# Expert weights from 64-column products, with the second one-hot stored tokens innermost

## The chip, the cores and the metric

The kernel runs on one core of a Trainium2 chip. The metric is device time in microseconds (us) from launch to end, taken as the median of several runs; the profile is one execution, taken by the hardware profiler, and shows the span from its first to its last instruction. Engines are named as in the profile: PE is TensorE's products, PEld its weight loads, DVE is VectorE, ACT is ScalarE, POOL is GpSimd and SP is SyncE. Lines are those of the kernel before, unless the text says otherwise.

## The reference, cut to what matters

The program is two transformer blocks over 256 tokens of width 1024. The first ends in a layer with 16384 small experts, laid out as a grid of 128 by 128. For each token and each of 8 heads, routing picks 16 experts, each by a pair of indices, and a softmax weight for each. So a token has 128 (index, index, weight) triples. The layer is

```python
z = jnp.einsum('thkd,td->thk', ub, hb)           # ub: the picked rows of u
a = (jax.nn.gelu(z.astype(jnp.float32)) * gb).astype(hb.dtype)
return jnp.einsum('thk,thkd->td', a, jnp.take(v, eb, axis=0))
```

All values are float32.

## The kernel before, in words

The kernel gathers nothing. It computes z for all experts densely, in 128 chunks of 128 experts by 256 tokens (`z_chunks`, line 1201: the weights of a chunk are loaded, split into a high and a low part by ACT, line 166, and DVE, line 167, and 24 products of 256 columns give z, lines 190 to 192; ACT applies the gelu on the way out of PSUM, line 987). A chunk has one second index and all 128 first indices on the partitions. The z of 32 chunks stand in one tile, a slice, so there are four slices, 0 to 3. Each z is multiplied by its expert's weight for that token, which is zero nearly everywhere, and `out_chunks` then multiplies the result with v, chunk by chunk, in products of 512 columns (lines 261 to 263, after another split by lines 268 and 269).

The weights come from `weights_of(s, n)`, which makes those of n slices from slice s on: it is called with (0, 1), (1, 2) and (3, 1). It goes over the tokens in 32 blocks of TB = 8. For each token the weight matrix, first index by second index, is a product over the token's 128 triples, which lie on the partitions: the one-hot of the first index, times the one-hot of the second index scaled by the weight. Both are f16; the weight g is split into a high and a low f16 part (i = 0 and 1, `gT`), so that two products, added up in PSUM, keep its precision. A block does this:

- DVE compares a table of numbers `io16` with the first indices and writes the one-hot `os`, tokens innermost (line 1166); ACT turns it to `o1`, one token's 128 columns in a row (line 1169).
- DVE compares `row16`, a row of the numbers 0 to 127, with the second indices and writes `o2`, tokens outermost (line 1172): m = 32 n columns a token.
- DVE multiplies `o2` with both parts of the weight into `og` (line 1176).
- PE does, for each of the 8 tokens and both parts, a weight load of `o1` and a product of m columns (line 1191) into the bank `g`, of which there are two.
- DVE multiplies z in place with what stands in the bank, one instruction a slice (line 1194).

`weights_of` is a generator that yields after making a block's operands and after the block's products; the operands are made one block ahead. The loops over chunks advance it: 1.5 steps a chunk while the chunks 50 to 95 of z are computed (slice 0), 1.05 while the first 32 chunks go out and the last 32 of z are computed (slices 1 and 2), and 1.05 while chunks 32 to 95 go out (slice 3). The engines run their instructions in the order in which they were recorded, so a block's instructions stand between those of the chunks. In `spread` (line 1111 and 1112) DVE writes the two parts of the weight to `gT`, tokens outermost. Line 973 fills `row16` once from `io16`, and the small product in `spread` (line 1099) puts the weights in order; neither is in the blocks.

Of the kernel before, what the change touches and what calls it, by code (L numbers as in the profile page):

```python
# [8 lines left out]
F32 = mybir.dt.float32  # L9
F32R = mybir.dt.float32r  # L10
F16 = mybir.dt.float16
# [3 lines left out]
ALU = mybir.AluOpType  # L15
# [7 lines left out]
TB = 8  # L23
# [90 lines left out]
def body(ctx: ExitStack, tc: tile.TileContext, a: dict):  # L114
    nc = tc.nc
    V, A, G, T, SY = nc.vector, nc.scalar, nc.gpsimd, nc.tensor, nc.sync

    def pool(name, space=None, stack=None, bufs=1):
        kw = {"space": space} if space else {}
        return (stack or ctx).enter_context(tc.tile_pool(name=name, bufs=bufs, reuse_waits="tile", **kw))  # L120
# [6 lines left out]
    def mmt(n=256):  # L127
        return pmm.tile([128, 512], F32, tag="mm", name="mm", bufs=2)[:, :n]
# [9 lines left out]
    def C(n, i=None, w=128):  # L138
        t, o, ww = CST[n]
        return cst[t][:, o:o + ww] if i is None else cst[t][:, o + i * w:o + i * w + w]  # L140
# [312 lines left out]
    with ExitStack() as p1:  # L453
# [320 lines left out]
        for t in ORD2.split():  # L774
            n = int(t[1])
# [86 lines left out]
        for j, w in enumerate(chunks(a["wo"], range(4))):  # L862
            ps = mmt()
# [12 lines left out]
        for j, w in enumerate(chunks(a["wga"], range(4))):  # L876
            ps = mmt()
# [18 lines left out]
        for j, w in enumerate(chunks(a["wgm"], range(4))):  # L896
            ps = mmt()
# [12 lines left out]
        for j in range(8):  # L910
            ps = mmt()
# [7 lines left out]
        for j in range(8):  # L919
            ps = mmt()  # L920
# [27 lines left out]
    with ExitStack() as p2:  # L948
        zp = pool("zp", stack=p2)
        zq = [zp, zp]  # L950
        m2 = pool("m2", stack=p2)
# [4 lines left out]
        def gt():  # L956
            return pgp.tile([128, 512], F32, tag="g", name="g", bufs=2)
# [10 lines left out]
        io16 = m2.tile([128, 128, TB], F16, name="io16")  # L968
        A.dma_start(out=io16, in_=a["io16"].rearrange("p (i t) -> p i t", t=TB))
        idxT = m2.tile([128, 2, 256], F16, name="idxT")  # L970
        gT = m2.tile([128, 256, 2], F16, name="gT")
        row16 = m2.tile([128, 128], F16, name="row16")
        V.tensor_copy(row16, io16[:, :, 0])

        rst = ExitStack()
        rp = pool("rp", stack=rst)
# [111 lines left out]
        def spread(t):  # L1088

            ex = rp.tile([128, 8, 16], F32, tag="ex", name="ex", bufs=2)  # L1090
            V.tensor_sub(ex, gw[t], gw[t][:, :, 0:1].to_broadcast([128, 8, 16]))
            A.activation(ex, ex, AF.Exp)
            sm = rp.tile([128, 2, 8], F32, tag="sm", name="sm", bufs=2)
            V.tensor_reduce(out=sm[:, 0, :], in_=ex, axis=AX.X, op=ALU.add)
            V.reciprocal(sm[:, 1, :], sm[:, 0, :])
            gp = rp.tile([128, 2, 16, 4], F32, tag="gp", name="gp", bufs=2)
            for q in range(2):
                hs = slice(4 * q, 4 * q + 4)
                V.tensor_mul(gp[:, q].rearrange("p k h -> p h k"), ex[:, hs],
                             sm[:, 1, hs, None].to_broadcast([128, 4, 16]))  # L1100
            yield 1.3
            ts_ = slice(t * 128, (t + 1) * 128)
            pt = gt()[:, :256]
            for i in range(2):
                T.transpose(pt[:, i * 128:(i + 1) * 128], fi[t][:, i, :], C("ident"))
            V.tensor_copy(idxT[:, :, ts_], pt.rearrange("p (i t) -> p i t", i=2))
            pg = gt()
            T.transpose(pg[:, 0:128], gp.rearrange("p q k h -> p (q k h)"), C("ident"))
            gs = rp.tile([128, 128], F32, tag="gs", name="gs", bufs=1)
            A.activation(gs, pg[:, 0:128], AF.Copy, scale=GS)  # L1110
            V.tensor_copy(gT[:, ts_, 0], gs)
            V.tensor_sub(gT[:, ts_, 1], gs, gT[:, ts_, 0])
            yield 1.0

        def routing():
            for hq in range(4):
                for t in range(2):
                    while (hq, t) not in scs:
                        yield
                    yield from route(t, hq, scs[hq, t])  # L1120
                if hq % 2:
                    for t in range(2):
                        yield from select(t, hq // 2)
                        if hq == 3:
                            yield from spread(t)
# [31 lines left out]
        def weights_of(s, n):  # L1157

            m = 32 * n

            def made_of(b):
                ts_ = slice(b * TB, (b + 1) * TB)
                os = op_.tile([128, 128, TB], F16, tag="os", name="os", bufs=1)
                V.tensor_tensor(out=os, in0=io16, in1=idxT[:, 0, None, ts_].to_broadcast([128, 128, TB]),  # L1166
                                op=ALU.is_equal)
                o1 = op_.tile([128, TB, 128], F16, tag="o1", name="o1", bufs=2)
                A.copy(o1, os.rearrange("p n t -> p t n"))  # L1169
                o2 = op_.tile([128, TB * 64], F16, tag="o2", name="o2", bufs=1)[:, :TB * m]  # L1170
                o2 = o2.rearrange("p (t n) -> p t n", t=TB)
                V.tensor_tensor(out=o2, in0=row16[:, None, 32 * s:32 * s + m].to_broadcast([128, TB, m]),
                                in1=idxT[:, 1, ts_, None].to_broadcast([128, TB, m]), op=ALU.is_equal)
                og = op_.tile([128, TB * 128], F16, tag="og", name="og", bufs=2)[:, :2 * TB * m]
                og = og.rearrange("p (t i n) -> p t i n", t=TB, i=2)
                V.tensor_tensor(out=og, in0=o2[:, :, None, :].to_broadcast([128, TB, 2, m]),  # L1176
                                in1=gT[:, ts_, :, None].to_broadcast([128, TB, 2, m]), op=ALU.mult)
                return o1, og

            blocks = S // TB  # L1180
            next_ = made_of(0)
            yield
            for b in range(blocks):
                o1, og = next_
                if b + 1 < blocks:
                    next_ = made_of(b + 1)
                    yield
                ps = gt()[:, :TB * m].rearrange("p (t n) -> p t n", t=TB)
                for t in range(TB):
                    for i in range(2):  # L1190
                        T.matmul(ps[:, t], lhsT=o1[:, t, :], rhs=og[:, t, i], start=i == 0, stop=i == 1)  # L1191
                for q_ in range(n):
                    zz = zt[s + q_][:, :, b * TB:(b + 1) * TB]
                    V.scalar_tensor_tensor(out=zz, in0=ps[:, :, 32 * q_:32 * q_ + 32].rearrange("p t n -> p n t"),  # L1194
                                           scalar=1.0 / GS, in1=zz, op0=ALU.mult, op1=ALU.mult)
                yield

# [36 lines left out]
        op_ = pool("op", stack=p2)  # L1234
        zq.append(op_)
        bg = [weights_of(0, 1)]
        z_chunks(ZR, 96, bg, NW)
        drain(bg)
        acc = [[pacc.tile([128, 512], F32, tag=f"acc{2 * t + c}", name="acc") for c in range(2)] for t in range(2)]
        rt = m2.tile([128, 2, 5], F32, name="rt")  # L1240

        bg = [weights_of(1, 2)]
        out_chunks(0, 32, bg, NX)
        z_chunks(96, 128, bg, NX)
        drain(bg)
        bg = [weights_of(3, 1)]
        out_chunks(32, 96, bg, NY)
        drain(bg)
# [10 lines left out]
    with ExitStack() as p3:  # L1259
# [48 lines left out]
        for j in range(8):  # L1308
            if j < 4:
                ps = pss[j]  # L1310
            else:
                ps = mmt()
# [53 lines left out]
        for j in range(4):  # L1366
            ps = mmt()
# [8 lines left out]
            for i in range(1, 4):  # L1376
                V.scalar_tensor_tensor(out=u2[:, j, :], in0=pad[:, i:i + 256], scalar=K("wc2", 4 * i + j),
                                       in1=u2[:, j, :], op0=ALU.mult, op1=ALU.add)
        gl = big("gl", F32, 4)
        for j in range(4):  # L1380
            ps = mmt()
# [7 lines left out]
            for i in range(2):  # L1389
                s_ = slice(64 * i, 64 * i + 64)  # L1390
                V.scalar_tensor_tensor(out=q2[s_, 2 * j + i, :], in0=qk[s_, j, :], scalar=lru[s_, 12:13],
                                       in1=rb[s_], op0=ALU.mult, op1=ALU.mult)
# [102 lines left out]
        for n in range(32):  # L1495
            if n < 4:
                ps = pss[n]
            else:
                ps = mmt()
# [139 lines left out]
```

## Time and profile before

| what | us |
|---|---|
| median of 3 runs (1453.45 to 1455.68) | 1454.52 |
| the profiled execution | 1454.12 |
| its span, first to last instruction | 1452.3 |
| PE busy | 1429.2 |
| PEld busy | 1312.1 |
| DVE busy | 1134.0 |
| ACT busy | 923.0 |

Busy time is the time in which at least one instruction of an engine was under way. PE's products overlap, since one starts before the one ahead of it has ended, so that a PE that is busy all the time need not be at its peak; the distance between the starts of two products says more than their duration. Idle time of an engine that is not the bottleneck costs nothing.

### The profile page before, as it was taken

The page shows a single profiled execution, that of the slowest core. Times are in us where ns is not written, and L with a number is a line of the kernel's source. Part 1 is how long each engine was busy: PE and PEld are TensorE (multiplying, and loading weights), DVE is VectorE, ACT ScalarE, POOL GpSimd, SP SyncE. Part 2 cuts the span into 40 slices and gives each one's busy share as a digit, 9 for nine tenths or more (in the row PEclk, how much of TensorE's full clock was granted, in tenths as well). Part 3 has the DMA queues.
Part 4 walks back from the last instruction along what each step waited for, and adds up shares of the span by engine and source line. Part 5 has one row for each costly group of instructions (what it writes and reads, how often), then busy time and mean ns, then how long its engine had stood idle before and what let it go on. Part 6 is the DMA issues. An engine that isn't in the chain of part 4 may idle for free.

```text
span 1452.3 us, 27093 instructions
## 1 busy us (share of the span) xinstructions
PE 1429.2 (98%) x10984; PEld 1312.1 (90%) x10984; DVE 1134.0 (78%) x2208; ACT 923.0 (64%) x1322; POOL 7.8 (1%) x11
## 2 busy tenths in 40 slices
PE   7999999999999999999999999999999999999998
PEld 6999999988999999998779997777788899989997
DVE  4979987668999878888998888888855778565554
ACT  4655565456444578887777777777744669454542
POOL 0000000010000000000000000000000000000000
PEclk9999999999999999999999999999999999999999
DMA  8757785553655555544545555555555543255552
GB/s 320 294 188 236 280 334 195 174 174 126 206 174 173 188 165 171 175 151 170 174 162 169 192 164 180 170 172 173 172 190 179 194 173 140 88 204 174 174 179 82
DMA packets 40301, 268.67 MB, mean 185 GB/s; under 512 B 4720, under 2 KB 5488, under 8 KB 9584
## 3 DMA queue, kind: packets, MB, share of 16 engines
q1 hardware_dynamic: 39168, 264.67, 52.9%
q10 hardware_dynamic: 1008, 2.27, 0.5%
q8 instruction: 86, 1.41, 0.4%
q14 instruction: 39, 0.32, 0.1%
HBM read 265.87 MB, written 1.05 MB: 184 GB/s over the span
## 4 chain that ended last, share of the span: by engine, by line
PE 92%; DVE 5%; ACT 2%; DMA 0%; issue 0%; DVEq 0%; SPq 0%; ACTq 0%
PE mm L190 16%; PE mm L192 15%; PE mm L191 15%; PE acc L261 11%; PE acc L262 11%; PE acc L263 11%; PE g L1191 3%; DVE wl L167 1%; DVE scr L471 1%; PE psb L606 1%; PE mm L226 1%; PE mm L225 1%; PE acc L190 1%; PE mm L230 1%; PE mm L209 1%; PE acc L192 1%
## 5 line engine op out<-in xcount | busy, mean ns | idle before, releaser
L166 ACT CAST wh<-raw 128x1024 fp32r<-128x1024 f32 x444 | 465.2, 1050 | 423.0 <-PE mm L191 217.9
L167 DVE TENSOR_TENSOR wl<-raw,wh 128x1024 fp32r<-128x1024 f32 x444 | 541.3, 1222 | 160.0 <-ACT wh L166 154.2
L190 PE MATMUL mm<-hh,wh 128*128 128x256 f32 x1800 | 512.7, 285 | 0.0
L192 PE MATMUL mm<-hh,wl 128*128 128x256 f32 x1800 | 507.2, 282 | 0.0
L191 PE MATMUL mm<-hl,wh 128*128 128x256 f32 x1800 | 505.6, 281 | 0.0
L190 PEld LDWEIGHTS mm<-hh,wh 128*128 128x128 f32 x1800 | 339.2, 188 | 2.0
L191 PEld LDWEIGHTS mm<-hl,wh 128*128 128x128 f32 x1800 | 339.9, 189 | 0.9
L192 PEld LDWEIGHTS mm<-hh,wl 128*128 128x128 f32 x1800 | 340.2, 189 | 0.0
L261 PE MATMUL acc<-wh,ah 128*128 128x512 f32 x512 | 205.4, 401 | 0.0
L262 PE MATMUL acc<-wh,al 128*128 128x512 f32 x512 | 201.9, 394 | 0.0
L263 PE MATMUL acc<-wl,ah 128*128 128x512 f32 x512 | 201.5, 394 | 0.0
L1169 ACT COPY o<-os 128x1024 f16<-128x1024 f16 x96 | 196.8, 2050 | 0.0
L263 PEld LDWEIGHTS acc<-wl,ah 128*128 128x128 f32 x512 | 96.2, 188 | 22.3
L261 PEld LDWEIGHTS acc<-wh,ah 128*128 128x128 f32 x512 | 96.2, 188 | 20.7
L262 PEld LDWEIGHTS acc<-wh,al 128*128 128x128 f32 x512 | 96.1, 188 | 20.5
L1194 DVE SCALAR_TENSOR_TENSOR z<-g,z 128x256 f32<-128x256 f32 x128 | 51.2, 421 | 43.3 <-PE g L1191 43.2
L1166 DVE TENSOR_TENSOR os<-io,idxT 128x1024 f16<-128x1024 f16 x96 | 66.3, 691 | 23.2 <-ACT o L1169 22.4
L1176 DVE TENSOR_TENSOR og<-o,gT 128x512 f16<-128x512 f16 (+1 forms) x96 | 82.6, 860 | 0.1
L1191 PEld LDWEIGHTS <-o 128*128 128x128 f16 x1536 | 46.5, 96 | 15.4 <-issue 12.2
L1191 PE MATMUL g<-og,o 128*128 128x32 f16 (+1 forms) x1536 | 56.6, 182 | 0.0
L269 DVE TENSOR_TENSOR al<-z,ah 128x256 fp32r<-128x256 f32 x128 | 53.5, 419 | 1.1 <-ACT ah L268 1.1
L471 DVE SCALAR_TENSOR_TENSOR scr<-araw,crow 128x1024 f32<-128x1024 f32 x43 | 52.4, 1218 | 0.2
(449 smaller groups left out, 1854.4 us busy)
## 6 DMA issues: line engine op xcount, KB each, us to landing
raw<-in_uT_dram SPq DMA_DIRECT2D x64, 1024.0 KB, 4.9
raw<-in_ev_dram SPq DMA_DIRECT2D x64, 1024.0 KB, 4.9
araw<-in_wada_dram SPq DMA_DIRECT2D x16, 1024.0 KB, 4.9
raw<-in_wup_dram SPq DMA_DIRECT2D x16, 1024.0 KB, 4.9
raw<-in_wdn_dram SPq DMA_DIRECT2D x16, 1024.0 KB, 4.9
raw<-in_wcxb_dram SPq DMA_DIRECT2D x12, 1024.0 KB, 4.9
raw<-in_wout_dram SPq DMA_DIRECT2D x8, 1024.0 KB, 4.8
raw<-in_wq_dram SPq DMA_DIRECT2D x8, 1024.0 KB, 4.8
```

The source lines that it names most:

```text
L166: by.copy(wh, raw) if by is A else by.tensor_copy(wh, raw)
L167: last = on.tensor_sub(wl, raw, wh)
L190: T.matmul(ps, lhsT=wh, rhs=xh, start=start, stop=False, skip_group_check=skip)
L191: T.matmul(ps[:, :n], lhsT=wh, rhs=xl, start=False, stop=False, skip_group_check=skip)
L192: return T.matmul(ps, lhsT=wl, rhs=xh, start=False, stop=stop, skip_group_check=skip)
L261: T.matmul(acc[t][c], lhsT=xh[:, ts_], rhs=wh[:, cs], start=first and n == 0, stop=False)
L262: T.matmul(acc[t][c], lhsT=xl[:, ts_], rhs=wh[:, cs], start=False, stop=False)
L263: T.matmul(acc[t][c], lhsT=xh[:, ts_], rhs=wl[:, cs], start=False, stop=last and n == len(steps) - 1)
L471: return V.scalar_tensor_tensor(out=scr, in0=raw, scalar=0.5, in1=crow, op0=ALU.mult, op1=ALU.mult, accum_out=ada[:, j:j + 1])
L1169: A.copy(o1, os.rearrange("p n t -> p t n"))
L1176: V.tensor_tensor(out=og, in0=o2[:, :, None, :].to_broadcast([128, TB, 2, m]), in1=gT[:, ts_, :, None].to_broadcast([128, TB, 2, m]), op=A ...
L1191: T.matmul(ps[:, t], lhsT=o1[:, t, :], rhs=og[:, t, i], start=i == 0, stop=i == 1)
```

## The change

In all slices, `o2`, `og` and `gT` now stand with tokens innermost: `o2` is compared straight out of `io16`, `row16` is gone, and the multiplication by the weight is two instructions, one for each part. PE therefore reads one token's columns of `og` with a step of TB = 8 elements of f16.

In slices 0 and 3 (n = 1), one product a token now takes both parts of the weight beside each other, as 64 columns, where there were two products of 32 columns added up in PSUM. The two halves are added afterwards: ACT copies the second half out of PSUM to a tile `both`, DVE adds the first half to it, and the update of z reads `both`. In slices 1 and 2 (n = 2) there are two products of 64 columns, as before.

```diff
--- before.py
+++ after.py
@@ -968,9 +968,7 @@
         io16 = m2.tile([128, 128, TB], F16, name="io16")
         A.dma_start(out=io16, in_=a["io16"].rearrange("p (i t) -> p i t", t=TB))
         idxT = m2.tile([128, 2, 256], F16, name="idxT")
-        gT = m2.tile([128, 256, 2], F16, name="gT")
-        row16 = m2.tile([128, 128], F16, name="row16")
-        V.tensor_copy(row16, io16[:, :, 0])
+        gT = m2.tile([128, 2, 256], F16, name="gT")
 
         rst = ExitStack()
         rp = pool("rp", stack=rst)
@@ -1108,8 +1106,8 @@
             T.transpose(pg[:, 0:128], gp.rearrange("p q k h -> p (q k h)"), C("ident"))
             gs = rp.tile([128, 128], F32, tag="gs", name="gs", bufs=1)
             A.activation(gs, pg[:, 0:128], AF.Copy, scale=GS)
-            V.tensor_copy(gT[:, ts_, 0], gs)
-            V.tensor_sub(gT[:, ts_, 1], gs, gT[:, ts_, 0])
+            V.tensor_copy(gT[:, 0, ts_], gs)
+            V.tensor_sub(gT[:, 1, ts_], gs, gT[:, 0, ts_])
             yield 1.0
 
         def routing():
@@ -1168,13 +1166,14 @@
                 o1 = op_.tile([128, TB, 128], F16, tag="o1", name="o1", bufs=2)
                 A.copy(o1, os.rearrange("p n t -> p t n"))
                 o2 = op_.tile([128, TB * 64], F16, tag="o2", name="o2", bufs=1)[:, :TB * m]
-                o2 = o2.rearrange("p (t n) -> p t n", t=TB)
-                V.tensor_tensor(out=o2, in0=row16[:, None, 32 * s:32 * s + m].to_broadcast([128, TB, m]),
-                                in1=idxT[:, 1, ts_, None].to_broadcast([128, TB, m]), op=ALU.is_equal)
+                o2 = o2.rearrange("p (n t) -> p n t", t=TB)
+                V.tensor_tensor(out=o2, in0=io16[:, 32 * s:32 * s + m, :],
+                                in1=idxT[:, 1, None, ts_].to_broadcast([128, m, TB]), op=ALU.is_equal)
                 og = op_.tile([128, TB * 128], F16, tag="og", name="og", bufs=2)[:, :2 * TB * m]
-                og = og.rearrange("p (t i n) -> p t i n", t=TB, i=2)
-                V.tensor_tensor(out=og, in0=o2[:, :, None, :].to_broadcast([128, TB, 2, m]),
-                                in1=gT[:, ts_, :, None].to_broadcast([128, TB, 2, m]), op=ALU.mult)
+                og = og.rearrange("p (i n t) -> p i n t", i=2, t=TB)
+                for i in range(2):
+                    V.tensor_tensor(out=og[:, i], in0=o2, in1=gT[:, i, None, ts_].to_broadcast([128, m, TB]),
+                                    op=ALU.mult)
                 return o1, og
 
             blocks = S // TB
@@ -1185,13 +1184,24 @@
                 if b + 1 < blocks:
                     next_ = made_of(b + 1)
                     yield
-                ps = gt()[:, :TB * m].rearrange("p (t n) -> p t n", t=TB)
-                for t in range(TB):
-                    for i in range(2):
-                        T.matmul(ps[:, t], lhsT=o1[:, t, :], rhs=og[:, t, i], start=i == 0, stop=i == 1)
+                if n == 1:
+
+                    ps = gt()[:, :2 * TB * m].rearrange("p (t i n) -> p t i n", t=TB, i=2)
+                    for t in range(TB):
+                        T.matmul(ps[:, t], lhsT=o1[:, t, :], rhs=og[:, :, :, t], start=True, stop=True)
+                    both = op_.tile([128, TB, 32], F32, tag="both", name="both", bufs=1)
+                    A.copy(both, ps[:, :, 1])
+                    V.tensor_tensor(out=both, in0=ps[:, :, 0], in1=both, op=ALU.add)
+                    gs_ = [both]
+                else:
+                    ps = gt()[:, :TB * m].rearrange("p (t n) -> p t n", t=TB)
+                    for t in range(TB):
+                        for i in range(2):
+                            T.matmul(ps[:, t], lhsT=o1[:, t, :], rhs=og[:, i, :, t], start=i == 0, stop=i == 1)
+                    gs_ = [ps[:, :, 32 * q_:32 * q_ + 32] for q_ in range(n)]
                 for q_ in range(n):
                     zz = zt[s + q_][:, :, b * TB:(b + 1) * TB]
-                    V.scalar_tensor_tensor(out=zz, in0=ps[:, :, 32 * q_:32 * q_ + 32].rearrange("p t n -> p n t"),
+                    V.scalar_tensor_tensor(out=zz, in0=gs_[q_].rearrange("p t n -> p n t"),
                                            scalar=1.0 / GS, in1=zz, op0=ALU.mult, op1=ALU.mult)
                 yield
 
```

The order of PE's instructions in a block of slice 0, before, from the last product of a chunk to the first weight loads of the block (`o` is the turned one-hot, `g` the bank); 14 more pairs follow before the next product of a chunk.

```order
L192 MATMUL mm<-hh,wl 128x256
L1191 LDWEIGHTS o_6483
L1191 MATMUL g<-og,o_6483 128x32
L1191 LDWEIGHTS o_6483
L1191 MATMUL g<-og,o_6483 128x32
```

After the change, in the same place; 6 more pairs follow.

```order
L192 MATMUL mm<-hh,wl 128x256
L1191 LDWEIGHTS o_6481
L1191 MATMUL g<-og,o_6481 128x64
L1191 LDWEIGHTS o_6481
L1191 MATMUL g<-og,o_6481 128x64
```

A block of slice 0 has 16 pairs before and 8 after, at the same place between the chunks; the products are twice as wide.

ACT in slice 0, before: the cast `wh` of a chunk's weights, its gelu into `z`, and the turned one-hot `o` of a block.

```order
L166 CAST wh<-raw 128x1024
L987 ACTIVATE z<-mm 128x256
L166 CAST wh<-raw 128x1024
L987 ACTIVATE z<-mm 128x256
L1169 COPY o_6839<-os 128x1024
L166 CAST wh<-raw 128x1024
L987 ACTIVATE z<-mm 128x256
```

After:

```order
L166 CAST wh<-raw 128x1024
L985 ACTIVATE z<-mm 128x256
L166 CAST wh<-raw 128x1024
L985 ACTIVATE z<-mm 128x256
L1193 COPY both<-g 128x256
L1167 COPY o_6818<-os 128x1024
L166 CAST wh<-raw 128x1024
L985 ACTIVATE z<-mm 128x256
```

The copy to `both`, which waits for the block's products, stands between the gelu and the `o` of the next block.

DVE in slice 0, before: the update of z, `og` of the next block, the low part `wl` of a chunk's weights, the one-hot `os` and the second one-hot `o`.

```order
L1194 SCALAR_TENSOR_TENSOR z<-g,z 128x32x8
L1176 TENSOR_TENSOR og<-o_7131,gT 128x512
L167 TENSOR_TENSOR wl<-raw,wh 128x1024
L1166 TENSOR_TENSOR os<-io_3918,idxT 128x1024
L1172 TENSOR_TENSOR o_7188<-row_3922,idxT 128x256
L1194 SCALAR_TENSOR_TENSOR z<-g,z 128x32x8
```

After:

```order
L1170 TENSOR_TENSOR o_7285<-io_3918,idxT 128x256
L167 TENSOR_TENSOR wl<-raw,wh 128x1024
L1194 TENSOR_TENSOR both<-g,both 128x256
L1164 TENSOR_TENSOR os<-io_3918,idxT 128x1024
L1204 SCALAR_TENSOR_TENSOR z<-both,z 128x32x8
L1175 TENSOR_TENSOR og<-o_7285,gT 128x256 x2
```

The addition into `both` now stands ahead of `os` and the update of z, and the `og` of the next block behind all three.

## Rows read from the trace of the kernel before

**Rows 1.** The page: span, and busy time of the engines (share of the span, instructions).

```profile
span 1452.3 us, 27093 instructions
PE 1429.2 (98%) x10984; PEld 1312.1 (90%) x10984; DVE 1134.0 (78%) x2208; ACT 923.0 (64%) x1322; POOL 7.8 (1%) x11
```

**Rows 2.** The page: the chain that ended last, by engine.

```profile
PE 92%; DVE 5%; ACT 2%; DMA 0%; issue 0%; DVEq 0%; SPq 0%; ACTq 0%
```

**Rows 3.** Windows by stage: us, busy time of each engine, granted clock, DMA share, GB/s.

```profile
520.00:660.00 140.00, 140.00 (x1563) 138.62 (x1562) 114.88 (x171) 120.97 (x120) 0.00 (x0) 1.00 0.49 165
665.00:860.00 195.00, 195.00 (x1640) 174.32 (x1640) 178.63 (x251) 145.55 (x155) 0.00 (x0) 1.00 0.51 173
880.00:1052.00 172.00, 172.00 (x1172) 136.45 (x1171) 142.59 (x229) 132.54 (x142) 0.00 (x0) 1.00 0.52 173
```

**Rows 4.** Timeline of PE, slice 0: start us, us, engine, line, operation, operands, count.

```profile
642.33 0.28 PE L192 MATMUL mm<-hh,wl 128*128 128x256 f32 x1
642.45 0.56 PE L1191 MATMUL g<-og,o 128*128 128x32 f16 x16
642.87 0.36 PE L190 MATMUL mm<-hh,wh 128*128 128x256 f32 x1
643.07 0.28 PE L191 MATMUL mm<-hl,wh 128*128 128x256 f32 x1
```

**Rows 5.** Timeline of PE, one block of slices 1 and 2.

```profile
694.20 0.40 PE L263 MATMUL acc<-wl,ah 128*128 128x512 f32 x1
694.44 0.64 PE L1191 MATMUL g<-og,o 128*128 128x64 f16 x16
694.92 0.48 PE L261 MATMUL acc<-wh,ah 128*128 128x512 f32 x1
695.23 0.40 PE L262 MATMUL acc<-wh,al 128*128 128x512 f32 x1
```

**Rows 6.** Timeline of PE around one block of slice 3.

```profile
943.71 0.40 PE L262 MATMUL acc<-wh,al 128*128 128x512 f32 x1
943.94 0.40 PE L263 MATMUL acc<-wl,ah 128*128 128x512 f32 x1
...
944.91 0.39 PE L262 MATMUL acc<-wh,al 128*128 128x512 f32 x1
```

**Rows 7.** ACT groups by form: line, operation, operands, count | busy us, mean ns | idle before.

```profile
L166 ACT CAST wh<-raw 128x1024 fp32r<-128x1024 f32 x444 | 465.2, 1050 | 423.0 <-PE mm L191 217.9 <-PE acc L262 119.3 <-issue 55.9
L1169 ACT COPY o<-os 128x1024 f16<-128x1024 f16 x96 | 196.8, 2050 | 0.0
...
L268 ACT CAST ah<-z 128x256 fp32r<-128x256 f32 x128 | 51.0, 402 | 0.3 <-DVE z L1194 0.2
...
L1147 ACT COPY qT<-mm 128x256 f32<-128x256 f32 x12 | 4.4, 365 | 0.0
```

**Rows 8.** DVE groups by form, in the order of cost.

```profile
L1176 DVE TENSOR_TENSOR og<-o,gT 128x512 f16<-128x512 f16 x64 | 43.7, 682 | 0.1
L1176 DVE TENSOR_TENSOR og<-o,gT 128x1024 f16<-128x1024 f16 x32 | 38.9, 1217 | 0.0
...
L1172 DVE TENSOR_TENSOR o<-row,idxT 128x256 f16<-128x256 f16 x64 | 26.8, 419 | 0.0
L1172 DVE TENSOR_TENSOR o<-row,idxT 128x512 f16<-128x512 f16 x32 | 21.9, 686 | 0.0
...
L1054 DVE TENSOR_TENSOR pr<-pr 128x512 f16<-128x512 f16 x12 | 5.0, 421 | 0.2
...
L1054 DVE TENSOR_TENSOR pr<-pr 128x256 f16<-128x256 f16 x12 | 3.5, 288 | 0.2
...
L1142 DVE TENSOR_TENSOR u<-g,rr 128x256 f32<-128x256 f32 x2 | 0.8, 418 | 0.0
```

**Rows 9.** Lines 973 and 1099 by themselves: count, duration ns min/median/max, first and last start.

```profile
L973 DVE COPY row<-io x1: 277/277/277, 324.6 to 324.6; 128x128 f16<-128x128 f16 x1
...
L1099 DVE TENSOR_TENSOR gp<-ex,sm x4: 263/267/274, 492.3 to 509.0; 128x64 f32<-128x64 f32 x4
```

## The prediction, made before the change was run

> **What bounds the kernel now.** I read the page first. TensorE's queue is busy 98% of the 1452.3 us span [rows 1], and the chain of work that ended last is 92% PE [rows 2]. An average over stages can hide a stage with another limit, so next I cut windows over the three stretches in which the changed lines run: slice 0 (520 to 660 us), slices 1 and 2 (665 to 860) and slice 3 (880 to 1052). In each of them PE is busy for the whole window, at the full granted clock of 1.00 (its 2.4 GHz level), while DVE and ACT have time over: 114.9 and 121.0 us of 140, 178.6 and 145.6 of 195, 142.6 and 132.5 of 172 [rows 3]. So PE sets the time there, a nanosecond more or less on PE is a nanosecond of the span, and work on DVE or ACT costs nothing until one of them has none to spare.
>
> The timeline then gives what one block of eight tokens costs PE. A product's duration is its latency, since products overlap; what counts is the distance between starts. In slice 0, two starts of the large products with a block between them lie 643.07 − 642.33 = 0.74 us apart, where two ordinary steps of 0.12 take 0.24: a block costs **0.50 us**. Of it 642.87 − 642.45 = 0.42 us is the 16 products of 32 columns, 26 ns each, and 0.08 us is the change from one kind of product to the other [rows 4]. In slice 3 it is 944.91 − 943.94 − 2 × 0.23 = 0.51 us [rows 6], the same. In slices 1 and 2, with 64 columns, the 16 products take 694.92 − 694.44 = 0.48 us, **30 ns each**, and the block 695.23 − 694.20 − 2 × 0.23 = 0.57 us [rows 5]. There are 64 blocks of the first kind and 32 of the second by the counts in [rows 8].
>
> **The change part by part.** *One product for two.* In slices 0 and 3 each block now has 8 weight loads and 8 products of 64 columns, for 16 and 16 of 32. If a product of 64 columns starts every p us, the block costs 8p in place of 0.42 us; the 0.08 us of changing over stays.
>
> *The new step of the moving operand.* This is the term that decides. Up to now PE read og along n, element after element. After the change tokens are innermost, so one token's columns lie 8 elements of f16 apart, which is 16 bytes, in all four slices. In slices 1 and 2 the number of products stays at 16 of 64 columns and only this step changes: 16p in place of 0.48 us. Together: 64 × (8p − 0.42) + 32 × (16p − 0.48) us, which is **1024p − 42.2**. The change breaks even at p = 41 ns, or 0.64 ns a column.
>
> No row of before shows PE with such a step. The lower bound is that the step is free: p = 30 ns [rows 5], and 1024 × 0.030 − 42.2 = −11.5 us. For the upper bound I look for other engines that step by 16 bytes in SBUF. ACT's copy of the first one-hot (line 1169) reads os with just this step, 8 elements of f16, and takes 2050 ns for 1024 elements. ACT's ordinary casts take 1050 ns for 1024 and 402 for 256, so 0.84 ns an element; the copy needs 1.00 us more, **1.82 ns an element** [rows 7]. On DVE the write with a step of 16 bytes (line 1099, four f32) takes 267 ns for 64 elements, where the lines 1172 (419 ns for 256, 686 for 512) give a fixed 152 ns and 1.04 an element [rows 8]: (267 − 152) / 64 = 1.80 ns an element [rows 9]. Against it stands DVE's small copy at line 973, which reads with this step: 277 ns for 128 elements, (277 − 152) / 128 = 0.98 ns an element, no slower than DVE goes anyway [rows 9]. So two of three such rows end at 1.8 ns, whatever the engine's own rate. PE's own dense stream agrees with a limit of that size: an f32 product of 512 columns starts 0.23 us after the one before it [rows 6], which is 1.8 ns for each 16 bytes of a partition, and no row shows PE taking in f32 faster than that.
>
> I take ACT's 1.82 ns a column, since it is the nearest row: a read, with the same type and step. Then p = 64 × 1.82 = 116 ns, well above what the weight load beside it needs (26 ns for a whole pair [rows 4]), so PE's stream sets the distance. A block of slices 0 and 3 then costs 8 × 0.116 + 0.08 = 1.01 us in place of 0.50, one of slices 1 and 2 16 × 0.116 + 0.09 = 1.95 in place of 0.57. In all 1024 × 0.1165 − 42.2 = **+77 us**. The other ends stay for the range: DVE's 0.98 ns gives p = 63 ns and +22 us; a free step gives −11.5.
>
> The Trainium skill, Advanced Engine Details and Errata, section SBUF Cachelines, says that SBUF is read in lines of 16 bytes and that an engine needs at least two hits on a line to hide the access. ACT's doubled copy agrees with that. By it PE, with one hit a line, would be slowed too; taken as half rate it gives the second rival below.
>
> *DVE.* The second one-hot and the weighted copies should go twice as fast, as f16 operations with dense innermost runs do: line 1054 takes 288 ns for 256 elements and 421 for 512 [rows 8]. In slices 0 and 3 a block's one-hot goes from 419 to 288 ns, its copies from 682 to 2 × 288 = 576, and an addition out of PSUM comes in, 418 ns by line 1142: +181 ns, 64 times, +12 us [rows 8]. In slices 1 and 2 it is 686 to 421 and 1217 to 2 × 421: −640 ns, 32 times, −20 us. Both lie beside PE [rows 3] and cost nothing and bring nothing, unless PE were to become short. Should the fast form not be taken, slices 1 and 2 would cost 2 × 686 − 1217 = 0.16 us more a block, 5 us on DVE, which its 16 us over in that stage still cover.
>
> *ACT.* 64 copies out of PSUM of 256 elements, 365 ns by line 1147 [rows 7]: +23 us, half of it in slice 0, where ACT goes from 121.0 to 132.7 us. With PE slower by 16 us there, that is 133 of 156; covered. The new wait: this copy stands behind the gelu of the same chunk and waits for the block's products, and behind it on ACT stand the copy o of the next block and the next wh; on DVE the addition waits for it, and behind that os, the update of z and the og of the next block, for which PE waits. Cost here nothing, because PE's slower block lengthens the time in which all this must be done; if that cover is gone, it is the third rival. *The copy to row16* (277 ns) had nobody waiting and goes for nothing.
>
> **The sum.** The profiled execution took 1454.12 us, 0.4 below the median of the runs. 1454.1 + 77 = **1531 us**. About 0.2%, 2.9 us, is what a measurement of this kernel can tell from no change.
>
> **The rivals.**
> *A, the step is free to PE* (the other side): PE takes og's columns 16 bytes apart at the 30 ns of today. Place: the products of all 96 blocks; it decides below p = 41 ns. For it: DVE's copy at line 973 is not slowed [rows 9], and half as many loads and products in 64 blocks is a true saving. Against it: lines 1169 and 1099, and that PE would have to take a new 16 bytes every 0.42 ns, four times as often as its f32 stream does. Time: 1454.1 − 11.5 = 1442.6 us. Chance 0.20. The Trainium skill, SBUF — State Buffer, section Door 1: The DMA port swizzle, calls a step of up to 8 bf16 elements free, which would be this rival; ACT's 2050 ns at exactly this step speaks against it.
>
> *B, half rate*: the step costs PE a factor of two, as it does to ACT by its own rate (1.82 against 0.84), not a fixed time: p = 60 ns, 1024 × 0.060 − 42.2 = +19, 1473 us. It can't be told from the forecast by any row of before, since no other row has an engine as fast as PE with such a step. For the forecast I prefer the fixed time, as DVE and ACT, with different rates of their own, both end at 1.8. Chance 0.27.
>
> *C, about even*: p between 38 and 44 ns, or rival A with most of its gain lost to ACT. In slice 0 ACT would be busy 132.7 us while PE, with 32 × 0.18 us less, would need 134; then the chain block, copy, addition, update, og, next block has no room, and up to 6 us of the 11.5 come back as idle PE. 1448 to 1457 us. Chance 0.05, mostly inside 0.2%.
>
> **How the numbers follow.** Forecast 0.48, B 0.27, A 0.20, C 0.05. The range leaves out A alone: from 1452 (C) to 1545, the forecast with 2 ns a column in place of 1.82 (1024 × 0.128 − 42.2 = +89 us, 1543). The forecast's own range is 1515 to 1545. Faster by over 0.2%: A, 0.20. Within: C, 0.05. Slower: forecast and B, 0.75.
>
> **What would show it.** In the changed profile, the distance between the starts of the 64-column products in slices 1 and 2: 116 ns if the forecast holds (a burst of 16 in 1.9 us), 60 by B, 30 by A. PE stays busy through all three stages and the stages grow by 16, 44 and 16 us; DVE's one-hot and copies fall to 288 and 421 ns each; ACT's busy time grows by some 23 us and its share of each stage falls. A burst of 16 in 0.5 us makes the prediction wrong outright; PE idle in front of a block, with ACT or DVE as releaser, would mean that a new wait and not the step sets the time.

## The result, and the profile after

The changed kernel takes 1523.8 us, the kernel before 1454.4: a ratio of 1.0482 with a 95% interval of 1.047 to 1.0495, so it is slower by 69.4 us. The forecast was 1531.

The page of the changed kernel, span and busy times, answers to [rows 1]:

```profile
span 1522.3 us, 26309 instructions
PE 1499.5 (98%) x10472; PEld 1382.8 (91%) x10472; DVE 1133.0 (74%) x2367; ACT 947.3 (62%) x1386; POOL 7.8 (1%) x11
```

PE has 512 products fewer than before (10472 for 10984) and is busy 70 us longer. DVE's busy time hardly moved and ACT's grew by 24 us. On the chain that ended last, by engine and by line, the products of the blocks now take 4% and 4% of the span (lines 1191 and 1200 of the changed kernel, one for slices 0 and 3, one for slices 1 and 2); the page of before had 3% for both:

```profile
PE 93%; DVE 5%; ACT 2%; issue 0%; DMA 0%; DVEq 0%; SPq 0%; ACTq 0%
PE mm L192 15%; PE mm L190 15%; PE mm L191 15%; PE acc L262 10%; PE acc L261 10%; PE acc L263 10%; PE g L1200 4%; PE g L1191 4%; DVE wl L167 1%; PE psb L606 1%; DVE scr L471 1%; PE mm L226 1%; PE mm L225 1%; PE acc L190 1%; PE mm L230 1%; PE mm L209 1%
```

The windows over the three stages (columns as in [rows 3]; the stages are longer now, so their bounds moved):

```profile
520.00:677.00 157.00, 157.00 (x1331) 155.62 (x1330) 128.18 (x239) 132.69 (x157) 0.00 (x0) 1.00 0.44 151
682.00:905.00 223.00, 223.00 (x1528) 202.60 (x1527) 149.81 (x266) 140.22 (x146) 0.00 (x0) 1.00 0.42 142
925.00:1115.00 190.00, 190.00 (x940) 153.73 (x939) 155.96 (x296) 147.02 (x176) 0.00 (x0) 1.00 0.48 164
```

PE is still busy for the whole of each, at the full granted clock, and DVE and ACT have more time over than they had. So nothing new waits ahead of PE; PE itself needs longer. The timeline of PE tells for what. First a block of slice 0, then one of slices 1 and 2:

```profile
645.74 0.28 PE L192 MATMUL mm<-hh,wl 128*128 128x256 f32 x1
645.86 1.09 PE L1191 MATMUL g<-og,o 128*128 128x64 f16 x8
646.70 0.37 PE L190 MATMUL mm<-hh,wh 128*128 128x256 f32 x1
646.90 0.28 PE L191 MATMUL mm<-hl,wh 128*128 128x256 f32 x1
```

```profile
703.83 0.40 PE L263 MATMUL acc<-wl,ah 128*128 128x512 f32 x1
704.06 2.02 PE L1200 MATMUL g<-og,o 128*128 128x64 f16 x16
705.83 0.48 PE L261 MATMUL acc<-wh,ah 128*128 128x512 f32 x1
706.15 0.40 PE L262 MATMUL acc<-wh,al 128*128 128x512 f32 x1
```

In slice 0 the burst of 8 products takes 646.70 − 645.86 = 0.84 us, 105 ns each, where 16 products of half the width took 0.42 [rows 4]. In slices 1 and 2 the burst of 16 takes 705.83 − 704.06 = 1.77 us, **111 ns each**; the same products, as many and as wide, took 0.48 us, 30 ns each, in [rows 5]. A whole block, measured as before, is 646.90 − 645.74 − 0.24 = 0.92 us for 0.50, and 706.15 − 703.83 − 0.46 = 1.86 us for 0.57. That gives 64 × 0.42 + 32 × 1.29 = 68 us, nearly all of the 69.4.

The average over a burst hides how it is made up. Two rows from the same burst of 16 show its second product (the first of two in the row) and its last one:

```profile
704.16 0.41 PE L1200 MATMUL g<-og,o 128*128 128x64 f16 x2
705.78 0.30 PE L1200 MATMUL g<-og,o 128*128 128x64 f16 x1
```

From the second to the last it is (705.78 − 704.16) / 14 = **116 ns** from start to start. The first distance is only 704.16 − 704.06 = 0.10 us, and the next product of a chunk starts 705.83 − 705.78 = 0.05 us after the last one. So a burst is 0.09 us shorter than 116 ns times its products: 16 × 0.116 = 1.86 for 1.77, and 8 × 0.116 = 0.93 for 0.84. The 8 products by which the two bursts differ cost 1.77 − 0.84 = 0.93 us, 116 ns each.

DVE's groups by form in the changed kernel answer to [rows 8]:

```profile
L1204 DVE SCALAR_TENSOR_TENSOR z<-both,z 128x256 f32<-128x256 f32 x64 | 40.4, 632 | 0.0
...
L1175 DVE TENSOR_TENSOR og<-o,gT 128x256 f16<-128x256 f16 x128 | 31.6, 288 | 45.7 <-PE g L1191 45.2
...
L1194 DVE TENSOR_TENSOR both<-g,both 128x256 f32<-128x256 f32 x64 | 26.7, 417 | 0.0
...
L1204 DVE SCALAR_TENSOR_TENSOR z<-g,z 128x256 f32<-128x256 f32 x64 | 24.2, 420 | 59.5 <-PE g L1200 59.4
L1175 DVE TENSOR_TENSOR og<-o,gT 128x512 f16<-128x512 f16 x64 | 24.1, 417 | 0.1
...
L1170 DVE TENSOR_TENSOR o<-io,idxT 128x256 f16<-128x256 f16 x64 | 18.6, 291 | 2.0
...
L1170 DVE TENSOR_TENSOR o<-io,idxT 128x512 f16<-128x512 f16 x32 | 13.4, 419 | 0.0
```

The one-hots and the weighted copies run at the fast rate, 288 to 291 and 417 to 419 ns, as forecast. The first row was not forecast: the update of z takes 632 ns where it reads `both` from SBUF, and 420 where it reads the bank in PSUM.

### The profile page after: what moved, and what is told of

It is laid out like the page before. It is cut to its first block, busy times and chain, and to the rows that moved or that the text cites. A ratio compares the mean times of both kernels' runs of the same rounds, so it can differ in the third digit from the quotient of the medians.

```text
span 1522.3 us, 26309 instructions
## 1 busy us (share of the span) xinstructions
PE 1499.5 (98%) x10472; PEld 1382.8 (91%) x10472; DVE 1133.0 (74%) x2367; ACT 947.3 (62%) x1386; POOL 7.8 (1%) x11
## 4 chain that ended last, share of the span: by engine, by line
PE 93%; DVE 5%; ACT 2%; issue 0%; DMA 0%; DVEq 0%; SPq 0%; ACTq 0%
PE mm L192 15%; PE mm L190 15%; PE mm L191 15%; PE acc L262 10%; PE acc L261 10%; PE acc L263 10%; PE g L1200 4%; PE g L1191 4%; DVE wl L167 1%; PE psb L606 1%; DVE scr L471 1%; PE mm L226 1%; PE mm L225 1%; PE acc L190 1%; PE mm L230 1%; PE mm L209 1%
## 5 line engine op out<-in xcount | busy, mean ns | idle before, releaser
L1175 DVE TENSOR_TENSOR og<-o,gT 128x256 f16<-128x256 f16 (+1 forms) x192 | 55.7, 331 | 45.8 <-PE g L1191 45.2
L1191 PE MATMUL g<-og,o 128*128 128x64 f16 x512 | 69.6, 292 | 0.0
L1204 DVE SCALAR_TENSOR_TENSOR z<-g,z 128x256 f32<-128x256 f32 x64 | 24.2, 420 | 59.5 <-PE g L1200 59.4
L1200 PE MATMUL g<-og,o 128*128 128x64 f16 x512 | 64.5, 294 | 0.0
L1191 PEld LDWEIGHTS <-o 128*128 128x128 f16 x512 | 51.1, 112 | 10.2 <-issue 8.0
L1200 PEld LDWEIGHTS <-o 128*128 128x128 f16 x512 | 55.3, 114 | 5.1 <-issue 4.2
```

Source lines behind the costliest of these rows:

```text
L1191: T.matmul(ps[:, t], lhsT=o1[:, t, :], rhs=og[:, :, :, t], start=True, stop=True)
L1200: T.matmul(ps[:, t], lhsT=o1[:, t, :], rhs=og[:, i, :, t], start=i == 0, stop=i == 1)
```

## The experiments

Theory S says that PE's new step through og sets the price: each column that begins a new 16 bytes costs a fixed time. The 1.64 to 1.73 ns a column in the expectations are averages over a burst, 105 and 111 ns by 64 columns. Its rivals are that the price belongs to the product and not to its columns (P), that the new copy, addition and waits cost part (W), that two columns in 16 bytes are enough (H), that any step but dense is slow (N), and that the price grows with the step (Q). All kernels compute the whole of the reference. Times are medians, beside runs of the kernel before on the same chip.

**Paired products, og dense.** Against the changed kernel, `o2`, `og` and `gT` lie tokens outermost again, made as in the kernel before; the products of 64 columns, `both` and the addition stay:

```diff
-                og = og.rearrange("p (i n t) -> p i n t", i=2, t=TB)
+                og = og.rearrange("p (t i n) -> p t i n", t=TB, i=2)
...
-                        T.matmul(ps[:, t], lhsT=o1[:, t, :], rhs=og[:, :, :, t], start=True, stop=True)
+                        T.matmul(ps[:, t], lhsT=o1[:, t, :], rhs=og[:, t], start=True, stop=True)
```

> Slices 0 and 3 keep the paired product of 64 columns, the copy by ACT and the addition by DVE; o2, og and gT lie tokens outermost again, so PE reads og densely in all slices. Theory S (the 16-byte step sets the price, 1.64 to 1.73 ns a column): the products go back to 30 ns, a burst of 8 takes 0.24 us, and 64 x (0.24 - 0.42) = -11.5 us against the kernel before, 1443 us. Rival W (the copy, the addition and the waits they bring cost part of the +69 us): PE idles ahead of the blocks and the time stays above 1454; at most 6 us of the 11.5 given back in slice 0 would be 1449.

Measured: 1444.5 us against 1454.2, ratio 0.9933 (0.9919 to 0.9946). PE around a block of slice 0, and the windows over the three stages:

```profile
646.88 0.28 PE L192 MATMUL mm<-hh,wl 128*128 128x256 f32 x1
647.01 0.41 PE L1192 MATMUL g<-og,o 128*128 128x64 f16 x8
647.25 0.36 PE L190 MATMUL mm<-hh,wh 128*128 128x256 f32 x1
647.45 0.28 PE L191 MATMUL mm<-hl,wh 128*128 128x256 f32 x1
```

```profile
520.00:655.00 135.00, 135.00 (x1309) 133.63 (x1309) 128.04 (x199) 127.18 (x149) 0.00 (x0) 1.00 0.49 170
660.00:855.00 195.00, 194.54 (x1634) 173.85 (x1635) 179.82 (x255) 146.56 (x160) 0.00 (x0) 1.00 0.51 171
875.00:1042.00 167.00, 167.00 (x925) 131.28 (x923) 156.38 (x260) 138.56 (x172) 0.00 (x0) 1.00 0.52 177
```

The burst is 647.25 − 647.01 = 0.24 us, 30 ns a product, and the block costs 647.45 − 646.88 − 0.24 = 0.33 us in place of 0.50. So all of the loss was in the layout, and the pairing by itself is a gain of 9.7 us. W is nearly out: in slice 0 ACT and DVE are busy 127 and 128 of 135 us, and the three windows show PE idle for 0.46 us in all. That is the tail of one wait of 0.90 us, which begins between the first two windows, at the end of slice 0. ACT ahead of it, and PE (idle time before a row, and what ended it, in brackets):

```profile
656.54 0.38 ACT L1194 COPY both<-g 128x256 f32<-128x256 f32 x1 [0.16 <-PE mm L191]
657.08 2.10 ACT L1169 COPY o<-os 128x1024 f16<-128x1024 f16 x1 [0.17 <-DVE os L1166]
659.07 1.06 ACT L166 CAST wh<-raw 128x1024 fp32r<-128x1024 f32 x1
660.01 0.40 ACT L987 ACTIVATE z<-mm 128x256 f32<-128x256 f32 x1
```

```profile
659.28 0.28 PE L192 MATMUL mm<-hh,wl 128*128 128x256 f32 x1
660.46 0.38 PE L190 MATMUL mm<-hh,wh 128*128 128x256 f32 x1 [0.90 <-ACT z L987]
```

Two products that are otherwise 0.12 us apart start 660.46 − 659.28 = 1.18 us apart, so W has its place, and it costs 1.1 us.

**Tokens innermost, products not paired.** The branch for n = 1 is never taken:

```diff
-                if n == 1:
+                if n == 0:
```

> All slices keep tokens innermost, but slices 0 and 3 go back to two products of 32 columns a token, added up in PSUM, with no copy to both and no addition. Theory S: a column costs 1.64 to 1.73 ns however they are grouped, so a product of 32 starts every 53 to 57 ns, a block of slices 0 and 3 has 16 of them, 0.85 to 0.91 us, as much as 8 of 64: about 1524 us, as the changed kernel. Rival P (the price belongs to the product, 105 to 111 ns each whatever its width): 16 x 0.108 = 1.73 us a block, 64 x 0.89 = 57 us more, 1581. Rival W: without the copy and the addition the part of slices 0 and 3 comes back, 27 us less, 1497.

Measured: 1529.3 us, ratio 1.052 (1.0504 to 1.0536). PE in a block of slice 0:

```profile
641.23 1.12 PE L1200 MATMUL g<-og,o 128*128 128x32 f16 x16
642.16 0.36 PE L190 MATMUL mm<-hh,wh 128*128 128x256 f32 x1
```

The second product of the same burst (the first of four in the row) and its last:

```profile
641.27 0.42 PE L1200 MATMUL g<-og,o 128*128 128x32 f16 x4
642.11 0.24 PE L1200 MATMUL g<-og,o 128*128 128x32 f16 x1
```

The 16 products of 32 columns take 642.16 − 641.23 = 0.93 us, 58 ns each: half as many columns cost about half as much, against P. Within the burst it is (642.11 − 641.27) / 14 = 60 ns from start to start. From 60 ns for 32 columns to 116 for 64 it is 56 / 32 = **1.75 ns a column, and 4 ns a product**. A burst of 16 products of 32 therefore costs a little more than one of 8 of 64, 0.93 us for 0.84, which is 64 × 0.09 = 6 us in all and about the difference to the changed kernel. Without the copy and the addition the time is not shorter; W is out here too.

**A step of 8 bytes.** `o2` and `og` in groups of 4 tokens, products paired:

```diff
-                og = og.rearrange("p (i n t) -> p i n t", i=2, t=TB)
+                og = og.rearrange("p (i h n t) -> p i h n t", i=2, h=2, t=4)
...
-                        T.matmul(ps[:, t], lhsT=o1[:, t, :], rhs=og[:, :, :, t], start=True, stop=True)
+                        T.matmul(ps[:, t], lhsT=o1[:, t, :], rhs=og[:, :, t // 4, :, t % 4], start=True, stop=True)
```

> As the changed kernel, but o2 and og lie in groups of 4 tokens, tokens innermost within a group: one token's columns are 8 bytes apart, two in each 16 bytes. Theory S (a fixed time for each new 16 bytes, shared by the columns that lie in it): 0.83 ns a column, p = 53 to 57 ns, 1024 x 0.055 - 42.2 = +14 us, 1468. Rival H (two columns in 16 bytes are enough for full speed): p = 30, 1443. Rival N (any step but dense is slow): p = 108, 1524.

Measured: 1470.6 us, ratio 1.0118 (1.0102 to 1.0133). PE in a block of slices 1 and 2:

```profile
696.52 1.12 PE L1201 MATMUL g<-og,o 128*128 128x64 f16 x16
697.45 0.48 PE L261 MATMUL acc<-wh,ah 128*128 128x512 f32 x1
```

The burst of 16 is 0.93 us, 58 ns each. These are 64 columns on 32 lines of 16 bytes, and they cost what 32 columns on 32 lines cost in the kernel ahead of this one: PE pays for the line, not for the column. That is S, at the upper end of the 53 to 57 ns that the expectation had, and against H and N.

**A step of 4 bytes.** The same with groups of 2 (`h=4, t=2`).

> As before, in groups of 2 tokens: 4 bytes apart, four columns in each 16 bytes. Theory S: 0.42 ns a column, which is PE's own rate, p = 30 ns, -11.5 us, 1443. Rival H: 1443 too. Rival N: 1524. DVE: if its fast form needs a longer innermost run than 2, o2 and og take 419 and 686 ns again instead of 288 and 421, hidden beside PE in all theories.

Measured: 1445.3 us, ratio 0.9937 (0.9922 to 0.9953). PE in a block of slices 1 and 2, and DVE's second one-hot:

```profile
701.47 0.65 PE L1201 MATMUL g<-og,o 128*128 128x64 f16 x16
701.95 0.48 PE L261 MATMUL acc<-wh,ah 128*128 128x512 f32 x1
```

```profile
L1170 DVE TENSOR_TENSOR o<-io,idxT 128x256 f16<-128x256 f16 x64 | 24.5, 382 | 2.0
...
L1170 DVE TENSOR_TENSOR o<-io,idxT 128x512 f16<-128x512 f16 x32 | 19.8, 618 | 0.0
```

The burst of 16 is 0.48 us, 30 ns each, as dense. With four columns a line a product crosses 16 lines, and 16 × 1.75 + 4 = 32 ns is within 2 ns of what the dense product takes anyway, so next to nothing is left to pay. The expectation on DVE was right in that the one-hot became slower, and wrong on why: it compares with two of every eight elements of `io16`, two to a line, and needs 618 − 382 = 236 ns for 256 elements or 128 lines, 1.84 ns a line. The copies into `og`, whose runs are just as short but dense, stay at 288 and 418 ns.

**A step of 32 bytes,** in slices 0 and 3, with half of `og`'s tile unused:

```diff
-                og = op_.tile([128, TB * 128], F16, tag="og", name="og", bufs=2)[:, :2 * TB * m]
-                og = og.rearrange("p (i n t) -> p i n t", i=2, t=TB)
+                og = op_.tile([128, TB * 128], F16, tag="og", name="og", bufs=2)
+                og = og.rearrange("p (i n t) -> p i n t", i=2, n=m)[:, :, :, 0:TB]
```

> As the changed kernel, but in slices 0 and 3 og is stored with 16 elements a column of which 8 are used, so PE steps by 32 bytes there; slices 1 and 2 keep 16 bytes. Theory S (a fixed time for each new 16 bytes, 1.64 ns): a column still begins one new 16 bytes, so the burst of 8 stays at 0.84 us and the time at 1524. Rival Q (the price grows with the step): 8 bytes gave 58 ns and 16 gave 111 a product, so 32 would give some 216, 8 x 0.106 = 0.85 us more in each of 64 blocks, +54 us, 1578.

Measured: 1524.7 us, ratio 1.0486 (1.047 to 1.0502). PE in a block of slice 0:

```profile
640.64 1.10 PE L1191 MATMUL g<-og,o 128*128 128x64 f16 x8
641.49 0.37 PE L190 MATMUL mm<-hh,wh 128*128 128x256 f32 x1
```

The burst of 8 is 0.85 us for 0.84 at 16 bytes. Past one line a column, the step costs no more; Q is out.

**ACT's copy at 8 bytes,** in the kernel before, with `os` alone in groups of 4:

```diff
-                os = op_.tile([128, 128, TB], F16, tag="os", name="os", bufs=1)
+                os = op_.tile([128, 2, 128, 4], F16, tag="os", name="os", bufs=1)
...
-                A.copy(o1, os.rearrange("p n t -> p t n"))
+                A.copy(o1.rearrange("p (h t) n -> p h t n", t=4), os.rearrange("p h n t -> p h t n"))
```

> The kernel before, with os alone stored in groups of 4 tokens, so that ACT's copy to o1 reads with a step of 8 bytes in place of 16. Theory S taken over to ACT: 512 new lines of 16 bytes at 1.82 ns and its fixed 186 ns give 1.12 us in place of 2.05. Rival R (turning the tile, or f16, is what makes this copy slow): 2.05 us as before. The time stays within 0.2% of before in both, 1454, since ACT is beside PE; if ACT's queue does set something in slice 0, up to 3 us less.

Measured: 1454.8 us, ratio 1.0005 (0.9995 to 1.0014). ACT's copy:

```profile
L1170 ACT COPY o<-os 128x1024 f16<-128x1024 f16 x96 | 107.6, 1120 | 0.0
```

1120 ns for 2050, as worked out from 512 lines at 1.82 ns. The copy that the prediction took its price from was slow by its step; with 4 bytes, in the next run, it is down to 1048 ns, the time of ACT's dense casts of that size [rows 7]. And taking 89 us off ACT, which is what 96 copies saved, is worth nothing here, since ACT is beside PE.

**All long steps taken out.** The version with groups of 2, with `os` in groups of 2 as well, a table of pairs for both one-hots, and `both` stored second index first:

```diff
+        io2 = m2.tile([128, 128, 2], F16, name="io2")
+        V.tensor_copy(io2, io16[:, :, 0:2])
...
-                    A.copy(both, ps[:, :, 1])
-                    V.tensor_tensor(out=both, in0=ps[:, :, 0], in1=both, op=ALU.add)
+                    A.copy(both, ps[:, :, 1].rearrange("p t n -> p n t"))
+                    V.tensor_tensor(out=both, in0=ps[:, :, 0].rearrange("p t n -> p n t"), in1=both, op=ALU.add)
```

> The version with groups of 2 tokens (1445.3 us) with the other long steps taken out as well: os in groups of 2 and compared against a table of pairs, so that ACT reads with 4 bytes; o2 compared against the same table; both stored second index first, so that the update of z reads it in order. Theory S: ACT's copy to o1 1.05 us in place of 2.06, DVE's o2 288 and 421 ns in place of 382 and 618, the update of z after both 420 in place of 635. All of it lies beside PE: the time is 1443 to 1445. If waits in slice 0 hold back the last part of the gain (9.0 us measured of 11.5 worked out), they go here: 1442.7. If the freed time of DVE and ACT is worth something by itself, it is below 1442.

Measured: 1443.9 us, ratio 0.9929 (0.9915 to 0.9942). ACT's copy, three of DVE's groups, and the windows:

```profile
L1170 ACT COPY o<-os 128x1024 f16<-128x1024 f16 x96 | 100.6, 1048 | 0.0
```

```profile
L1208 DVE SCALAR_TENSOR_TENSOR z<-both,z 128x256 f32<-128x256 f32 x64 | 26.7, 418 | 0.0
...
L1173 DVE TENSOR_TENSOR o<-io,idxT 128x256 f16<-128x256 f16 x64 | 18.6, 291 | 2.0
...
L1173 DVE TENSOR_TENSOR o<-io,idxT 128x512 f16<-128x512 f16 x32 | 13.4, 417 | 0.0
```

```profile
520.00:655.00 135.00, 135.00 (x1306) 133.63 (x1305) 114.91 (x231) 96.41 (x150) 0.00 (x0) 1.00 0.50 172
660.00:855.00 195.00, 195.00 (x1637) 174.32 (x1636) 157.09 (x283) 113.89 (x156) 0.00 (x0) 1.00 0.51 172
875.00:1042.00 167.00, 167.00 (x925) 131.54 (x924) 144.48 (x288) 111.83 (x172) 0.00 (x0) 1.00 0.53 177
```

Every duration came out as expected, and ACT is busy 96 us in slice 0 where the paired dense version had 127. The time is within a microsecond of that version's 1444.5: PE fills the windows, and the paired dense version's wait of 0.90 us on ACT's gelu at the end of slice 0 (0.34 us in the version with groups of 2) is gone. In those two versions PE waited for nothing else between 515 and 1060 us, so this is all that the time freed on DVE and ACT could buy, and a microsecond can't be told from noise here. The three versions of this section that read og densely or by 4 bytes beat both kernels, by 9 to 10 us against before and by 79 to 80 against the change.

## Why the prediction was right, point by point

*What bounds the kernel.* Right: PE is the whole of the three stages before and after [rows 3], and changes of tens of microseconds on DVE and ACT (the last two experiments) left the time where it was, but for a microsecond at most.

*One product for two.* Right: with og dense the burst of 8 takes the 0.24 us that 30 ns a product give, and the pairing saves 9.7 us of the 11.5 that were the sum's. The blocks by themselves give 64 × 0.17 = 11 us, and 1.1 us of it goes again in PE's wait on ACT's gelu. That is near to rival C, which had ACT run short and allowed it up to 6 us; but PE did not wait ahead of a block for the chain that C names, it waited for the gelu, ahead of which the copy, `o` and `wh` stand on an ACT with little time to spare.

*The new step.* Right in kind: the price is a fixed time for each 16 bytes and not a factor on the engine's own rate, shown by 111, 58 and 30 ns at 16, 8 and 4 bytes, and by no change at 32. Rival B, at 60 ns, and rival A, at 30, have no block in the changed kernel. The distance between starts came out as forecast, 116 ns for 64 × 1.82 [rows 7]. That it did so to the nanosecond is luck, since PE's own price is 1.75 ns a line and 4 ns a product, and ACT's row only lay near it. What the sum had too high is the burst: it took 8 and 16 products to last 8p and 16p, and every burst was 0.09 us shorter, by its first product and its last. That is 96 × 0.09 = 9 us, the whole of the difference between +77 and the 68 us of the blocks; by their blocks the stages grew by 32 × 0.42 = 13, 41 and 13 us, where 16, 44 and 16 were forecast. Why the ends of a burst are cheaper was not tried. The 1.8 ns for a line of PE's dense f32 stream proved nothing, since it may as well be the time of four columns.

*Against line 973.* The prediction set aside this one row, a copy on DVE that reads with the same step at 0.98 ns an element [rows 9]. Two rows of the runs stand on the other side, DVE's one-hot out of `io16` at 1.84 ns a line (the run with 4 bytes) and the update of z out of `both` at (632 − 152) / 256 = 1.88. The last run has a second such copy, which fills its table of pairs:

```profile
L971 DVE COPY io<-io x1: 274/274/274, 324.9 to 324.9; 128x256 f16<-128x256 f16 x1
```

It takes twice as many elements from the same 128 lines in the same time, 274 ns for 277. So this copy seems to pay by the line too, at 0.98 ns, about half of what the two others pay; these are single executions, no run has a dense copy of that size, and why it is half stays open.

*The rule on lines of 16 bytes.* The Trainium skill, Advanced Engine Details and Errata, section SBUF Cachelines, asks for at least two hits a line. For ACT the runs agree nearly: with two, the copy takes 1120 ns, with four 1048. For PE they differ, and the measurement decides: with two columns a line a product takes 58 ns, and only with four 30. The step of 8 bf16 elements that the Trainium skill, SBUF — State Buffer, section Door 1: The DMA port swizzle, calls free is the step of f16 elements, just as wide, that cost all of the 69 us.

*DVE.* The fast forms came as forecast. The update of z was priced unchanged, and took 212 ns more when it read `both` from SBUF by steps of 128 bytes: 64 × 0.21 = 14 us on DVE that the sum did not have. They were covered by PE, as everything there was. *ACT.* 64 copies of 369 ns, for 365 forecast; the wait for the block's products showed nowhere as idle PE in the changed kernel, where PE's slower blocks covered it, as the prediction said; without that cover, in the paired dense version, PE stood idle for the 0.90 us above.

## What to carry to other kernels

Count the lines of 16 bytes that an operand crosses, not its elements: an engine that is fast for each element loses most, here PE a factor of 3.7 (1.77 us for 0.48 a burst) where ACT lost 2 on the same step. If one engine wants a transposed layout for its fast form, give it runs that fill enough of a line for the fastest reader; groups of 2 f16 tokens kept DVE's fast form and PE's full rate at once. And when no row of a trace shows an engine under a new access, look for another engine that already does it, and ask whether its loss is a factor or a fixed time before carrying it over. A price from start to start is not yet the price of a burst: the first product and the last can cost less.

## What the runs showed that I had not expected

The same step of 128 bytes cost DVE nothing in PSUM and 212 ns in SBUF. In the kernel before, the update of z reads the bank with this step in slices 0 and 3 and takes 421 ns:

```profile
L1194 DVE SCALAR_TENSOR_TENSOR z<-g,z 128x256 f32<-128x256 f32 x128 | 51.2, 421 | 43.3 <-PE g L1191 43.2
```

It takes 632 from `both`, with the same shape and order, and 418 once `both` is stored in reading order. And the constants of three engines lie close together though their own rates do not: a new line of 16 bytes costs PE 1.75 ns (and 4 ns a product), ACT 1.82 and DVE, in instructions with two inputs, 1.84 to 1.88.
